# Output product of an FFN in two-row half-blocks: token combinations on another engine, plain rows in eight units, additions one unit later, rotary tables made in an earlier stage

## The chip, the cores and the metric

The kernel runs on one core of a Trainium2 chip. The metric is the time of one execution on the device in microseconds. A core has five engines that work side by side and wait for one another by semaphores: TensorE (PE, matrix products; PEld is its loading of weights), VectorE (DVE), ScalarE (ACT), GpSimd (POOL) and SyncE (SP, here used to issue transfers). Each runs its own instructions in order. Transfers between DRAM and the on-chip memory (SBUF) are issued by SP and, here, by POOL, and are carried out by DMA engines. Matrix products are summed up in PSUM, which is divided into banks; one bank holds a tile of 128 x 512 float32.

## What is computed

The reference is a trunk of two layers on x (512 tokens of 1024 float32 numbers). Layer 0 is a Conformer convolution module, layer 1 native sparse attention (queries, keys and values with a partial rotary embedding of the positions), and each is followed by a SwiGLU FFN of 2816 hidden numbers:

```python
x = x + conformer_conv_module(rmsnorm(x))
x = x + swiglu_ffn(rmsnorm(x))
x = x + nsa_attention(rmsnorm(x), positions)
x = x + swiglu_ffn(rmsnorm(x))

def swiglu_ffn(h, w_in, w_out):
    gate, up = jnp.split(h @ w_in, 2, axis=-1)
    return (jax.nn.silu(gate) * up) @ w_out
```

The rotary embedding takes the cosine and sine of `positions * inv_freq`, with `inv_freq = ROPE_THETA ** (-arange(8) / 8)`.

## The kernel before

Everything is kept transposed: x is eight tiles `x[m]` of 128 numbers by 512 tokens. A float32 product is made of three faster ones: each operand is split into a high part (rounded to the type fp32r) and the remainder, and high x high, high x low and low x high are summed in PSUM (`mm3`, lines 276 to 279). The weights are split on the chip: `next_w` (L229) asks for raw weights on SP's queue up to three units ahead (`w_dma`, L207; three buffers), ACT copies the high part (`w_hi`, L217), DVE subtracts it (`w_lo`, L226). High and low part have two buffers each, so a unit's split can be written only when the unit two before has been used.

The change is in the last stage of `ffn` (from L951), y times `w_out`. The 2816 rows of `w_out` are 22 blocks of 128. Eight of them, the plain rows (`EARLY` and `LATE`, four each), are multiplied as they stand. The other 14 are two halves of seven (`NO`), and with the two halves of the outputs and the two halves (256 tokens each) of the tokens they make a 2 x 2 block product, which the kernel forms with seven products in place of eight (Strassen's way). They come in the order `OUT_SEQ` = 1, 4, 2, 3, 5, 6, 7; each is 28 blocks of 128 x 128 weights, cut into four units u of 8, 8, 8 and 4 blocks, and a block is three matmuls of 256 columns. "(4,1)" below is unit 1 of product 4. Products 1, 4 and 7 use raw weights. The others use sums of two quarters of the weights, formed by DMA: `s_base` (L1029, SP's queue) loads one, `s_more` (L1033, POOL's queue) accumulates another upon it, and ACT and DVE split the sum (`soh` L1040, `sol` L1041).

The token operands are split too: `direct` (L992 to L996) for a quarter of y, `summed` (L1001, L1002) for a combination of quarters, which is formed by `z_1`, `z_4` (both through `z_new`, L1007) and `z_on` (L1020, in place), on POOL. `divide` (L757 to L761) splits the plain rows of y.

The results lie in PSUM. `bank()` hands out the six banks of the pool `fpm`; another pool, `fpa`, has two. For each of the four row blocks j of a product, `AD[j]` is a bank held from product 1 to product 7, `B[j]` one held during product 4. `out_add` (L1069 to L1076) adds a finished result to its half of x on DVE. When a tile of x is final, `finish_x` (L323) prepares the next layer: high part on ACT (L311), low part on DVE (L312), square on ACT, sum of the squares on POOL (the last on DVE).

The order is written out by hand. Plain rows come first: four units P0 to P3, each two tiles m by the four `EARLY` rows (`plain`, added to x by `keep_plain`, L962). The `LATE` rows are eight pieces of four blocks ("Q" slots), put between the units of the seven products by `LATE_AT` (L100) and made by `late` (L1118 to L1125) in a bank of `fpa`. `slots` lists the units, and the loop of L1142 does for each: ask for and split the weights of the next one, issue this unit's matmuls, do what `todo` lists for it (operands, transfers), then the additions that it has completed, and `finish_x`. Each engine keeps this order. The generator `rope_tables` (L1178) hands fourteen pieces of work on the rotary tables to the first FFN's `todo`: the load of the positions, DVE operations on 128 x 512 tiles and three ACT operations.

The convolution module ends with its own output product, for m = 0 to 7: addition to x (L719) and `finish_x`. The attention (`nsa`) takes the tables as arguments.

Of the kernel before, what the change touches and what calls it, by code (L numbers as in the profile page):

```python
# [19 lines left out]
P = 128  # L20
T = 512
# [78 lines left out]
LATE_AT = {(1, 1): (0,), (4, 0): (1,), (4, 2): (4,), (2, 0): (2,), (2, 2): (5,), (3, 0): (3,), (3, 2): (6,),  # L100
           (5, 1): (7,)}
# [16 lines left out]
def trunk(ctx: ExitStack, tc: tile.TileContext, A, out):  # L118
# [32 lines left out]
    def add_ffn(l):  # L151
# [5 lines left out]
        for i in range(4):  # L157
            add("fw_p", l * 4 + i, 1024)
        for z in OUT_SEQ:
            for u in range(QU):  # L160
                if z in OUT_RAW:
                    units.append(quarter(l, OUT_RAW[z], u))
                for m in LATE_AT.get((z, u), ()):
                    add("fw_r", l * NK + m, LATE * P)
# [221 lines left out]
    def proj_tile(pool, tag, xh=None, xl=None, mid=None, fixed=False):  # L386
# [16 lines left out]
        return ps  # L403


    def conv_module():
        acc = new_acc()
        with ExitStack() as cx:
# [307 lines left out]
            acc = new_acc()  # L716
            for m in range(NK):
                ps = pss[m] if m < 4 else proj_tile(po, "po", ah, al)
                nc.vector.tensor_tensor(x[m], x[m], ps, ALU.add)  # L719
                finish_x(m, V_NF0, acc, fin(m))  # L720
        return acc


    def ffn(acc, gnext, layer, between=None):
# [9 lines left out]
        with ExitStack() as cx:  # L734
# [219 lines left out]
            def plain(m):  # L954
                wh, wl = w
                pss[m] = bank()
                for f in range(EARLY):
                    c = slice(m % 2 * EARLY * P + f * P, m % 2 * EARLY * P + (f + 1) * P)
                    mm3(pss[m], wh[:, c], wl[:, c], ah[f], al[f], f == 0, f == EARLY - 1)
# [8 lines left out]
            plain(0)  # L968
# [35 lines left out]
            def z_new(name, g, a, b):  # L1004
                z = zs[name, g] = fo.tile([P, len(PAIRS[g]) * H], F32, tag=f"{name}{g}", name=nm("z"))
                for k, i in enumerate(PAIRS[g]):
                    pe(nc.gpsimd.tensor_tensor(z[:, k * H:(k + 1) * H], half(*a(i)), half(*b(i)), ALU.subtract))  # L1007
# [7 lines left out]
            def z_on(g, t, op):  # L1015
                z = zs["zz", g]
                for k, i in enumerate(PAIRS[g]):
                    c = slice(k * H, (k + 1) * H)
                    ab = (z[:, c], half(1, i, t)) if op == ALU.add else (half(1, i, t), z[:, c])
                    pe(nc.gpsimd.tensor_tensor(z[:, c], *ab, op))  # L1020
# [64 lines left out]
            tables = list(between(fo)) if between else []  # L1085
# [9 lines left out]
            for g in range(NG):  # L1095
                at(("P", (0, 1, 1, 2, 2)[g]), L(direct, 1, g, "oA", 0, 0, -1.0))
                at(("P", (1, 1, 1, 2, 2)[g]), L(z_1, g))
                at((1, (0, 0, 1, 1, 2)[g]), L(z_4, g))
# [19 lines left out]
            def late(m, w):  # L1118
                wh, wl = w
                ps = pa.tile([P, T], F32, tag="pa", name=nm("late"))  # L1120
                for k in range(LATE):
                    f = EARLY + k
                    c = slice(k * P, (k + 1) * P)
                    mm3(ps, wh[:, c], wl[:, c], ah[f], al[f], k == 0, k == LATE - 1)
                pe(nc.vector.tensor_tensor(x[m], x[m], ps, ALU.add))  # L1125

            slots = [("P", n) for n in range(1, 4)]
# [8 lines left out]
            plain(1)  # L1136
            keep_plain(0)
            for f in todo.pop(("P", 0)):
                f()
            keep_plain(1)  # L1140
            ready = None
            for n, (p, u) in enumerate(slots):  # L1142
# [877 lines left out]
```

## Time and profile before

| | |
|---|---|
| device time, three runs | 1276.36, 1276.45 and 1273.76 us, median 1276.36 |
| the profiled execution, its own time | 1270.59 us |
| its span, from the first to the last instruction | 1268.7 us |
| PE busy | 1211.6 us, 95% of the span |
| DVE busy | 916.5 us, 72% |
| ACT busy | 603.0 us, 48% |
| POOL busy | 413.9 us, 33% |
| output stage of the first FFN (417.70 to 552.40 us) | 134.70 us, PE busy 120.62, DVE 100.49, POOL 46.40 |
| output stage of the second FFN (1136.00 to 1265.40 us) | 129.40 us, PE busy 118.99, DVE 88.56, POOL 33.40 |

The profile belongs to one execution, which was faster than the three timed ones; its rows add up to its own time. An engine's busy time doesn't count instructions that only issue a transfer. "idle before <- X" in a row is the time that an engine stood before an instruction, with the instruction whose end released it. Numbers after an x are counts; "128x1024 fp32r<-128x1024 f32" is a tile written and a tile read, partitions by elements. L1063 is the matmul of `products`, `st` and `late` are PSUM tiles, `wl` and `wh` the low and high part of raw weights, `sol` and `soh` those of summed weights, `oz` a split token operand, `z` a combination of tokens, `al` and `ah` the parts of plain rows of y.

### The profile page before, as it was taken

What the parts mean: (1) busy time and instruction counts of PE and PEld (TensorE: products, weight loads), DVE (VectorE), ACT (ScalarE), POOL (GpSimd) and SP (SyncE); (2) the same over time, 40 slices, a digit from 0 to 9 for tenths busy, and PEclk for the clock granted to TensorE, in tenths of its full rate; (3) what the DMA queues carried; (4) which work ended last, traced back from release to release, by engine and by line L of the source; (5) the groups of instructions that cost most, each with busy time, mean ns of one, the idle gap of its engine ahead of it and who ended that gap; (6) DMA issues with size and microseconds to landing.
All of it is one profiled execution on the core that took longest, in us unless ns stands there. A gap on an engine that the chain in (4) does not pass through costs nothing.

```text
span 1268.7 us, 22185 instructions
## 1 busy us (share of the span) xinstructions
PE 1211.6 (95%) x8519; PEld 1047.5 (83%) x8519; DVE 916.5 (72%) x1604; ACT 603.0 (48%) x1124; POOL 413.9 (33%) x482
## 2 busy tenths in 40 slices
PE   9999999999999989889998999999999999998988
PEld 6787788899999888777777766668879999997878
DVE  6995678787666686755687887654597877767665
ACT  5221454455555344533443777753354544543433
POOL 2010030144443332332332566542212444442320
PEclk9999999999999999999999999999999999999999
DMA  8747635367774679154266011002534666638852
GB/s 312 259 147 257 174 111 160 112 170 211 186 181 127 182 200 182 26 171 114 58 143 167 18 34 26 3 15 68 184 105 142 175 175 174 175 104 224 197 124 84
DMA packets 89530, 180.06 MB, mean 142 GB/s; under 512 B 36880, under 2 KB 38544, under 8 KB 87888
## 3 DMA queue, kind: packets, MB, share of 16 engines
q1 hardware_dynamic: 68688, 112.48, 28.1%
q0 software_dynamic: 20736, 66.17, 23.2%
q8 instruction: 67, 1.10, 0.4%
q14 instruction: 39, 0.32, 0.1%
HBM read 165.08 MB, written 5.28 MB: 134 GB/s over the span
## 4 chain that ended last, share of the span: by engine, by line
PE 63%; DVE 12%; issue 10%; POOL 6%; ACT 4%; DMA 2%; SPq 2%; POOLq 0%; DVEq 0%; ACTq 0%
PE st L859 15%; PE st L1063 8%; PE pp L279 6%; PE pp L277 6%; PE pp L278 6%; PE O L1759 3%; PE cpe L515 2%; DVE wl L226 2%; POOL S L834 2%; PE pv L1594 2%; POOL S L833 2%; PE T L1733 1%; DVE sol L1041 1%; POOL S L826 1%; PE S L1702 1%
## 5 line engine op out<-in xcount | busy, mean ns | idle before, releaser
L217 ACT ACTIVATE wh<-wr 128x1024 fp32r<-128x1024 f32 (+3 forms) x158 | 154.2, 976 | 223.4 <-PE pp L278 60.8
L226 DVE TENSOR_TENSOR wl<-wr,wh 128x1024 fp32r<-128x1024 f32 (+3 forms) x158 | 186.6, 1181 | 32.0 <-ACT wh L217 31.4
L859 PE MATMUL st<-bh,sh 128*128 128x256 f32 x680 | 194.1, 285 | 3.5 <-DVE t L884 3.5
L859 PE MATMUL st<-bh,sl 128*128 128x256 f32 x680 | 192.5, 283 | 1.1 <-DVE sl L843 1.1
L859 PE MATMUL st<-bl,sh 128*128 128x256 f32 x680 | 192.0, 282 | 0.0
L277 PE MATMUL pp<-hh,wh 128*128 128x512 f32 x400 | 158.9, 400 | 3.7 <-ACT wh L217 3.6
L279 PE MATMUL pp<-hh,wl 128*128 128x512 f32 x400 | 157.6, 397 | 4.4 <-DVE wl L226 4.4
L278 PE MATMUL pp<-hl,wh 128*128 128x512 f32 x400 | 158.0, 396 | 0.0
L843 DVE TENSOR_TENSOR sl<-S,sh 128x512 fp32r<-128x512 f32 x136 | 111.8, 859 | 55.2 <-ACT sh L842 54.2
L859 PEld LDWEIGHTS st<-bh,sh 128*128 128x128 f32 x680 | 129.8, 191 | 5.8 <-DVE t L884 4.1
L859 PEld LDWEIGHTS st<-bh,sl 128*128 128x128 f32 x680 | 130.1, 191 | 1.5 <-DVE sl L843 1.5
L859 PEld LDWEIGHTS st<-bl,sh 128*128 128x128 f32 x680 | 130.5, 192 | 0.1
L1720 POOL TENSOR_SCALAR Pm<-Pm,sm,gates 128x512 f32<-128x512 f32 (+3 forms) x128 | 80.8, 643 | 59.9 <-DVE sm L1716 47.2
L833 POOL TENSOR_TENSOR S<-S,wr 128x512 f32<-128x512 f32 x34 | 53.9, 1586 | 134.1 <-DMA wr<-fw_in 71.6
L277 PEld LDWEIGHTS pp<-hh,wh 128*128 128x128 f32 x400 | 75.2, 188 | 24.6 <-ACT wh L217 6.0
L279 PEld LDWEIGHTS pp<-hh,wl 128*128 128x128 f32 x400 | 75.2, 188 | 24.0 <-DVE wl L226 6.9
L278 PEld LDWEIGHTS pp<-hl,wh 128*128 128x128 f32 x400 | 75.3, 188 | 18.0 <-issue 1.1
L842 ACT ACTIVATE sh<-S 128x512 fp32r<-128x512 f32 x136 | 79.2, 620 | 21.6 <-POOL S L833 21.5
L826 POOL DMA_DIRECT2D S<-fw_x x34 | 40.3, 1186 | 145.0 <-DMA S<-fw_x 143.9
L1706 ACT ACTIVATE Pm<-Pm,mx 128x512 f32<-128x512 f32 (+3 forms) x128 | 71.1, 557 | 34.1 <-DVE mx L1705 31.2
L1063 PE MATMUL st<-oz,soh 128*128 128x256 f32 x448 | 81.8, 284 | 0.5 <-ACT soh L1040 0.5
L1705 DVE CUSTOM_DVE_ANT_0 Pm<-S,mask 128x512 f32<-128x512 f32 (+3 forms) x128 | 59.2, 484 | 28.2 <-PE S L1703 27.6
(318 smaller groups left out, 3023.7 us busy)
## 6 DMA issues: line engine op xcount, KB each, us to landing
S<-fw_x POOLq DMA_DIRECT2D x68, 512.0 KB, 6.0
wr<-fw_in SPq DMA_DIRECT2D x46, 512.0 KB
bd<-bands POOLq DMA_DIRECT2D x12, 1280.0 KB, 12.8
So<-fw_q POOLq DMA_DIRECT2D x24, 512.0 KB, 5.9
wr<-fw_q SPq DMA_DIRECT2D x18, 512.0 KB
r<-fw_x SPq DMA_DIRECT2D x34, 256.0 KB
wr<-cw_in SPq DMA_DIRECT2D x14, 512.0 KB
So<-fw_q SPq DMA_DIRECT2D x12, 512.0 KB
```

Source lines behind the costliest of these rows:

```text
L217: parted(after(nc.scalar.activation(hi[:, :cols], raws[i][:, :cols], AF.Copy), pin.get(AF)))
L226: parted(after(nc.vector.tensor_tensor(lo[:, :cols], raws[i][:, :cols], hi[:, :cols], ALU.subtract), pin.get(ALU)))
L277: held(nc.tensor.matmul(ps, wh, xh, start=first, stop=False))
L278: held(nc.tensor.matmul(ps, wh, xl, start=False, stop=False))
L279: held(nc.tensor.matmul(ps, wl, xh, start=False, stop=last))
L833: pe(nc.gpsimd.tensor_tensor(t[:, :T], S[n][:, :T], w[:, :T], ALU.add))
L842: pe(nc.scalar.activation(h_[:, c], z, AF.Copy))
L843: pe(nc.vector.tensor_tensor(l_[:, c], z, h_[:, c], ALU.subtract))
L859: pe(nc.tensor.matmul(ps[:, :H], p_[:, k], m_[c][:, t], start=first and c == 0 and q == 0, stop=last and c == 3 and q == 2, skip_group_che ...
L1063: pe(nc.tensor.matmul(ps, a[:, c], b[:, t], start=p in (1, 4) and i == 0 and r == 0, stop=i == NO - 1 and r == 2, skip_group_check=True))
L1706: at_[AF] = nc.scalar.activation(Pt, Pt, AF.Exp, bias=mx, scale=-1.0, accum_out=sm)
L1720: nc.gpsimd.tensor_scalar(Pt, Pt, sm[:, k:k + 1], gates[:, t + k, br * 16 + h:br * 16 + h + 1], ALU.mult, ALU.mult)
```

## The change

1. `z_new` and `z_on` run on DVE: 28 operations of 128 x 256 per FFN.
2. The `late` pieces are gone. The plain rows are eight units of eight blocks (24 matmuls of 512): P0 has tiles 0 and 1 with rows 0 to 3, P1 tile 2 with rows 0 to 3 and tile 0 with rows 4 to 7, P2 tiles 1 and 2 with rows 4 to 7; then one unit for each tile 3 to 7 with all eight rows, placed by `PLAIN_AT` behind (4,1), (2,2), (3,0), (5,0) and (5,2). Each tile is added to x once, not twice: eight additions fewer per FFN. The weights are packed on the host to match. `divide` of rows 4 to 7 moves from P3 to P0.
3. Additions (`out_add`, `keep_plain`) are put into `behind` and issued one slot later, after the next unit's matmuls and `todo`; the last slot issues its own as well. `finish_x` follows them, and its sum of squares is on DVE.
4. `z_1` moves to P2, (1,0), (1,1), (1,2), `z_4` from product 1 to product 3, `direct` for product 1 to P1 and P2, half of the first `s_more` to (1,0).
5. The rotary tables are made in the output stage of the convolution module, three pieces after each of the tiles m = 3 to 7, in buffers of that stage (`uf`); the two results are written to DRAM (`angles`) and loaded again at the start of the attention. The positions and the two writes go by POOL's queue, the loads by SP's.

The PSUM pools and `bank()` are as before.

```diff
-LATE_AT = {(1, 1): (0,), (4, 0): (1,), (4, 2): (4,), (2, 0): (2,), (2, 2): (5,), (3, 0): (3,), (3, 2): (6,),
-           (5, 1): (7,)}
+PLAIN = [[(m, f) for m in range(a, b) for f in range(c, d)] for a, b, c, d in (
+    (0, 2, 0, 4), (2, 3, 0, 4), (0, 1, 4, 8), (1, 3, 4, 8), *((m, m + 1, 0, 8) for m in range(3, NK)))]
+PLAIN[1:3] = [PLAIN[1] + PLAIN[2]]
+PLAIN_AT = {(4, 1): 3, (2, 2): 4, (3, 0): 5, (5, 0): 6, (5, 2): 7}
...
+    angles = [tc.dram_tile([P, T], F32, name=nm("angle")) for _ in range(2)]
+
+    def rope_tables(new, follow):
+        pos = new(I32)
+        pf, n, sinT, cosT = (new(F32) for _ in range(4))
+        big = 1.5 * 2.0 ** 23
+        lim = 3.1415925
+
+        def g(name, *a):
+            return lambda: follow(getattr(nc.vector, name)(*a))
+
+        yield lambda: nc.gpsimd.dma_start(pos, A["positions"].partition_broadcast(P))
+        yield g("tensor_copy", pf, pos)
+        yield g("tensor_scalar", pf, pf, v(V_INVF), None, ALU.mult)
+        yield g("tensor_scalar", n, pf, 1.0 / (2.0 * math.pi), big, ALU.mult, ALU.add)
+        yield g("tensor_scalar", n, n, -big, None, ALU.add)
+        for c in _two_pi_pieces():
+            yield g("scalar_tensor_tensor", pf, n, -c, pf, ALU.mult, ALU.add)
+        yield g("tensor_scalar", pf, pf, lim, -lim, ALU.min, ALU.max)
+        yield lambda: (follow(nc.scalar.activation(sinT, pf, AF.Sin)), follow(nc.scalar.activation(n, pf, AF.Abs)),
+                       follow(nc.scalar.activation(cosT, n, AF.Sin, bias=halfpi, scale=-1.0)))
+        yield g("tensor_scalar", sinT, sinT, v(V_SGN), None, ALU.mult)
+        yield g("tensor_scalar", cosT, cosT, v(V_ISR), v(V_NISR), ALU.mult, ALU.add)
+        yield lambda: (nc.gpsimd.dma_start(angles[0], cosT), nc.gpsimd.dma_start(angles[1], sinT))
...
+            follow = dict(chain)
+
+            def table(dt):
+                return cp.tile([P, 8, 68], dt, tag="uf", bufs=len(PE_CONV), name=nm("tab")).rearrange(
+                    "p a b -> p (a b)")[:, :T]
+
+            tables = list(rope_tables(table, lambda z: after(z, follow[z.ins.engine])))
             for m in range(NK):
                 ps = pss[m] if m < 4 else proj_tile(po, "po", ah, al)
                 nc.vector.tensor_tensor(x[m], x[m], ps, ALU.add)
                 finish_x(m, V_NF0, acc, fin(m))
+                for _ in range(3 if m > 2 else 0):
+                    if tables:
+                        tables.pop(0)()
+            assert not tables
...
-            def plain(m):
+            def plain(w, blocks, k0=0):
                 wh, wl = w
-                pss[m] = bank()
-                for f in range(EARLY):
-                    c = slice(m % 2 * EARLY * P + f * P, m % 2 * EARLY * P + (f + 1) * P)
-                    mm3(pss[m], wh[:, c], wl[:, c], ah[f], al[f], f == 0, f == EARLY - 1)
+                for k, (m, f) in enumerate(blocks, k0):
+                    if m not in pss:
+                        pss[m] = bank()
+                    c = slice(k * P, (k + 1) * P)
+                    mm3(pss[m], wh[:, c], wl[:, c], ah[f], al[f], f == 0, f == EARLY + LATE - 1)
...
-                    pe(nc.gpsimd.tensor_tensor(z[:, k * H:(k + 1) * H], half(*a(i)), half(*b(i)), ALU.subtract))
+                    pe(nc.vector.tensor_tensor(z[:, k * H:(k + 1) * H], half(*a(i)), half(*b(i)), ALU.subtract))
...
-                    pe(nc.gpsimd.tensor_tensor(z[:, c], *ab, op))
+                    pe(nc.vector.tensor_tensor(z[:, c], *ab, op))
...
-                at(("P", (0, 1, 1, 2, 2)[g]), L(direct, 1, g, "oA", 0, 0, -1.0))
-                at(("P", (1, 1, 1, 2, 2)[g]), L(z_1, g))
-                at((1, (0, 0, 1, 1, 2)[g]), L(z_4, g))
+                at(("P", (1, 1, 2, 2)[g]), L(direct, 1, g, "oA", 0, 0, -1.0))
+                at((("P", 2), (1, 0), (1, 1), (1, 2))[g], L(z_1, g))
+                at((3, g), L(z_4, g))
...
-                at(("P", 3), L(divide, f, fo))
+                at(("P", 0), L(divide, f, fo))
...
-                at(("P", 2 + u // 2), L(s_more, 0, u))
+                at(("P", 2) if u < 2 else (1, 0), L(s_more, 0, u))
...
+            behind = []
+            slots = [("P", n) for n in range(1, 3)]
             for p in OUT_SEQ:
                 for u in range(QU):
                     slots.append((p, u))
-                    slots.extend(("Q", m) for m in LATE_AT.get((p, u), ()))
-            for n, f in enumerate(tables):
-                at(slots[1 + n], f)
+                    if (p, u) in PLAIN_AT:
+                        slots.append(("P", PLAIN_AT[p, u]))
...
-                if p == "Q":
-                    late(u, w)
-                    for f in todo.pop((p, u), ()):
-                        f()
-                    continue
+                sums_ = behind[:]
+                behind.clear()
                 if p == "P":
-                    plain(2 * u)
-                    plain(2 * u + 1)
-                    done = []
+                    plain(w, PLAIN[u])
+                    behind.extend(lambda m=m: keep_plain(m) for m, f in PLAIN[u] if f == EARLY + LATE - 1)
                 else:
-                    done = products(p, u, w)
+                    for j in products(p, u, w):
+                        behind.append(lambda p=p, j=j: out_add(p, j))
                 for f in todo.pop((p, u), ()):
                     f()
-                if p == "P":
-                    keep_plain(2 * u)
-                    keep_plain(2 * u + 1)
-                for j in done:
-                    out_add(p, j)
+                if n + 1 == len(slots):
+                    sums_ += behind
+                for f in sums_:
+                    f()
                 while finals:
                     m = finals.pop(0)
-                    finish_x(m, gnext, acc, fin(m))
+                    finish_x(m, gnext, acc, nc.vector)
...
+        tabs = []
+        for i in range(2):
+            t = rp.tile([P, T], F32, name=f"tab{i}")
+            nc.sync.dma_start(t, angles[i])
+            tabs.append(t)
+        cosT, sinT = tabs
...
-        fp.append(w[:EARLY].reshape(EARLY, P, 4, 2, P).transpose(2, 1, 3, 0, 4).reshape(4, P, 1024))
-        fr.append(w[EARLY:EARLY + LATE].transpose(2, 1, 0, 3).reshape(NK, P, LATE * P))
+        fp.extend(np.concatenate([w[f, :, m] for m, f in z], 1)[None] for z in PLAIN)
```

More of the change, by code (lines that the diff above doesn't have):

```diff
@@ L156, in add_ffn @@
             add("fw_in", l * n + i, 1024)
-        for i in range(4):
-            add("fw_p", l * 4 + i, 1024)
+        for i in range(3):
+            add("fw_p", l * NK + i, 1024)
         for z in OUT_SEQ:
@@ L162, in add_ffn @@
                     units.append(quarter(l, OUT_RAW[z], u))
-                for m in LATE_AT.get((z, u), ()):
-                    add("fw_r", l * NK + m, LATE * P)
+                if (z, u) in PLAIN_AT:
+                    add("fw_p", l * NK + PLAIN_AT[z, u], 1024)
     add_ffn(0)
@@ L720, in conv_module, with ffn @@
                 finish_x(m, V_NF0, acc, fin(m))
+                for _ in range(3 if m > 2 else 0):
+                    if tables:
+                        tables.pop(0)()
+            assert not tables
         return acc
-    def ffn(acc, gnext, layer, between=None):
+    def ffn(acc, gnext, layer):
         gcol = (V_NF0, V_NF1)[layer]
@@ L966, in split_next @@
                 w_lo()
-            plain(0)
+            plain(w, PLAIN[0][:4])
             split_next()
@@ L1083, in out_add @@
                     finals.append(m)
-            tables = list(between(fo)) if between else []
             NG = len(PAIRS)
@@ L1116, in ffn @@
                 at((4, u), L(s_more, 3, u))
[L1118 to L1127, printed above, removed]
+            behind = []
+            slots = [("P", n) for n in range(1, 3)]
             for p in OUT_SEQ:
@@ L1130, in ffn @@
                     slots.append((p, u))
-                    slots.extend(("Q", m) for m in LATE_AT.get((p, u), ()))
-            for n, f in enumerate(tables):
-                at(slots[1 + n], f)
+                    if (p, u) in PLAIN_AT:
+                        slots.append(("P", PLAIN_AT[p, u]))
             acc = new_acc() if gnext is not None else None
-            plain(1)
-            keep_plain(0)
+            plain(w, PLAIN[0][4:], 4)
             for f in todo.pop(("P", 0)):
                 f()
-            keep_plain(1)
             ready = None
@@ L1175, in ffn, with nsa @@
         return acc
-    rope = []
-    def rope_tables(fo):
+    def nsa(acc, gnext):
+        cx = ExitStack()
         rp = hx[0].enter_context(tc.tile_pool(name="rp", bufs=1))
-        cosT = rp.tile([P, T], F32, name="cosT")
-        sinT = rp.tile([P, T], F32, name="sinT")
-        rope.extend((cosT, sinT))
-        pf, n = (fo.tile([P, T], F32, name=z) for z in ("posf", "ropen"))
-        pos = fo.tile([P, T], I32, name="pos")
-        g = nc.vector
-        big = 1.5 * 2.0 ** 23
-        lim = 3.1415925
-        yield lambda: held(nc.sync.dma_start(pos, A["positions"].partition_broadcast(P)))
-        yield lambda: held(g.tensor_copy(pf, pos))
-        yield lambda: held(g.tensor_scalar(pf, pf, v(V_INVF), None, ALU.mult))
-        yield lambda: held(g.tensor_scalar(n, pf, 1.0 / (2.0 * math.pi), big, ALU.mult, ALU.add))
-        yield lambda: held(g.tensor_scalar(n, n, -big, None, ALU.add))
-        for c in _two_pi_pieces():
-            yield lambda c=c: held(g.scalar_tensor_tensor(pf, n, -c, pf, ALU.mult, ALU.add))
-        yield lambda: held(g.tensor_scalar(pf, pf, lim, -lim, ALU.min, ALU.max))
-        yield lambda: (held(nc.scalar.activation(sinT, pf, AF.Sin)), held(nc.scalar.activation(n, pf, AF.Abs)),
-                       held(nc.scalar.activation(cosT, n, AF.Sin, bias=halfpi, scale=-1.0)))
-        yield lambda: held(g.tensor_scalar(sinT, sinT, v(V_SGN), None, ALU.mult))
-        yield lambda: held(g.tensor_scalar(cosT, cosT, v(V_ISR), v(V_NISR), ALU.mult, ALU.add))
-    def nsa(acc, cosT, sinT, gnext):
-        cx = ExitStack()
+        tabs = []
[4 more added lines that the diff above has]
+        cosT, sinT = tabs
         def pool(cxx, name, bufs, **kw):
@@ L1856, in trunk @@
     cx0.close()
-    acc = ffn(acc, V_NM1, 0, rope_tables)
-    cosT, sinT = rope
-    acc = nsa(acc, cosT, sinT, V_NF1)
+    acc = ffn(acc, V_NM1, 0)
+    acc = nsa(acc, V_NF1)
     ffn(acc, None, 1)
@@ L1965, in _layout @@
     o["cw_os"], o["cw_o"] = start_units(co[:, :T]), tiles(co[:, T:])
-    fs, fi, fx, fp, fq, fr = [], [], [], [], [], []
+    fs, fi, fx, fp, fq = [], [], [], [], []
     for l in range(2):
@@ L1982, in _layout @@
     o["fw_s"], o["fw_in"], o["fw_x"] = np.concatenate(fs), np.concatenate(fi), np.concatenate(fx)
-    o["fw_p"], o["fw_q"], o["fw_r"] = np.concatenate(fp), np.concatenate(fq), np.concatenate(fr)
+    o["fw_p"], o["fw_q"] = np.concatenate(fp), np.concatenate(fq)
     w = f["nsa_w_in"][0]
```

## The prediction

> **What bounds the kernel now.** The execution whose page I read took 1270.59 us around this span:
> ```profile
> span 1268.7 us, 22185 instructions
> ```
> TensorE (PE) is nearly always busy, so a change pays only where PE waits. The change touches the output product of both FFNs (417–552 and 1136–1265 us) and the rotary tables. There I asked first for PE's waits by releaser (columns: total, count, longest), in the first FFN from 441 to 517, then from 517 to 556, then in the second FFN from 1160 to 1266:
> ```profile
> PE st L1063 <- DVE wl L226: 4.2, 2, 3.6
> PE st L1063 <- DVE sol L1041: 3.0, 3, 1.9
> ```
> ```profile
> PE st L1063 <- DVE sol L1041: 3.2, 3, 1.1
> PE st L1063 <- DVE wl L226: 2.0, 3, 0.9
> PE pp L279 <- DVE wl L226: 1.3, 1, 1.3
> PE pp L277 <- ACT wh L217: 1.1, 1, 1.1
> PE st L1063 <- ACT soh L1040: 0.5, 2, 0.3
> ```
> ```profile
> PE st L1063 <- DVE sol L1041: 5.7, 4, 4.0
> PE st L1063 <- DVE wl L226: 4.7, 3, 3.4
> ```
> All name the low half of a split weight, made on VectorE (DVE). Next the timeline at the longest waits (start, length, instruction, idle before). First FFN, start of product 1: PE, GpSimd (POOL), DVE:
> ```profile
> 448.29 0.58 PE L1063 MATMUL st<-oz,wl 128*128 128x256 f32 x1 [3.57 <-DVE wl L226]
> ```
> ```profile
> 439.21 5.20 POOL L1007 TENSOR_TENSOR z<-y,y 128x256 f32<-128x256 f32 x7
> ```
> ```profile
> 438.08 7.49 DVE L761 TENSOR_TENSOR al<-y,ah 128x512 fp32r<-128x512 f32 x4
> ```
> Second FFN, start of product 6:
> ```profile
> 1229.55 0.58 PE L1063 MATMUL st<-oz,sol 128*128 128x256 f32 x1 [3.99 <-DVE sol L1041]
> ```
> ```profile
> 1223.25 5.15 POOL L1020 TENSOR_TENSOR z<-y,z 128x256 f32<-128x256 f32 x7
> ```
> ```profile
> 1224.81 4.68 DVE L1041 TENSOR_TENSOR sol<-So,soh 128x1024 fp32r<-128x1024 f32 x1 [0.17 <-ACT soh L1040]
> ```
> Each time POOL combines operands while a DVE subtraction is stretched. What DVE operations take otherwise, from the groups of the first FFN's stage (last columns: busy, mean ns, idle before):
> ```profile
> L1041 DVE TENSOR_TENSOR sol<-So,soh 128x1024 fp32r<-128x1024 f32 x12 | 17.1, 1423 | 4.4 <-ACT soh L1040 4.4
> L226 DVE TENSOR_TENSOR wl<-wr,wh 128x1024 fp32r<-128x1024 f32 x12 | 15.3, 1274 | 5.0 <-ACT wh L217 5.0
> L1076 DVE TENSOR_TENSOR x<-x,st 128x256 f32<-128x256 f32 x27 | 11.1, 413 | 2.0 <-PE st L1063 2.0
> L226 DVE TENSOR_TENSOR wl<-wr,wh 128x512 fp32r<-128x512 f32 x11 | 9.1, 827 | 1.2 <-ACT wh L217 1.2
> L1002 DVE TENSOR_TENSOR oz<-z,oz 128x512 fp32r<-128x512 f32 x12 | 7.9, 681 | 0.0
> L761 DVE TENSOR_TENSOR al<-y,ah 128x512 fp32r<-128x512 f32 x4 | 7.5, 1932 | 0.0
> L1125 DVE TENSOR_TENSOR x<-x,late 128x512 f32<-128x512 f32 x8 | 5.5, 684 | 5.9 <-PE late L279 5.9
> ```
> `al` takes 1.93 us where a subtraction of that size takes 0.68, and one `sol` took 4.68 where the mean is 1.42. POOL needs 5.20/7 = 0.74 us per combination. The Trainium skill, "SBUF — State Buffer", section "SBUF: two separate sides", says that VectorE operations with two SBUF inputs and GpSimd operations that read SBUF exclude one another for a whole instruction, the loser blocking fully; the trace agrees in direction (1.93 against 0.68).
>
> The waits also cost clock. Windows of 15 us behind the waits of 3.4, 3.57 and 3.99 us (granted clock in the third column from the end, then DMA share):
> ```profile
> 1160.00:1175.00 15.00, 11.59 (x87) 10.84 (x86) 12.88 (x21) 5.45 (x12) 2.50 (x4) 1.00 0.84 256
> 448.00:463.00 15.00, 14.05 (x94) 13.30 (x95) 12.24 (x26) 4.74 (x7) 0.43 (x1) 0.89 0.88 255
> 1229.00:1244.00 15.00, 14.45 (x96) 13.73 (x96) 9.17 (x15) 4.50 (x7) 0.00 (x0) 0.89 0.25 87
> ```
> The chain of waits shows like units behind a slow and a normal start:
> ```profile
> 448.29 4.19 PE st L1063 x22
> ...
> 460.40 2.88 PE st L1063 x22
> ```
> So a slow clock costs 4.19 − 2.88 = 1.3 us, after 3.57 and 3.99, not after 3.4.
>
> **The change, part by part: what goes.** (1) The 28 combinations of an FFN move from POOL to DVE. PE's waits beside POOL fall: 3.57 and, at product 5 (longest of the `sol` waits, 1.9), down to the 0.5 that its two neighbours have ((3.0 − 1.9)/2): 1.4. Second FFN: 3.4, and 4.0 down to 0.5: 3.5. Together 11.9. (2) The two slow starts: 2.6. (3) The end of the first FFN: five wait groups of 8.1 us, in which the split of the new x (`finish_x`) stands ahead of weight splits. With additions and `finish_x` one unit later, the last unit's 0.9 and the next layer's 1.3 and 1.1 stay, others go but for about nothing: 8.1 − 3.3 = 4.8. In the last slot two tiles' `finish_x` fall together; I count 0 for that, at most the 0.8 of a subtraction. What goes: 19.3. (4) The matmuls stay, only cut into other units. Eight additions of 0.68 per FFN go, off PE's path, and make room for (1): a combination on DVE is 0.37 us by this row of the same shape:
> ```profile
> 208.16 0.75 DVE L796 TENSOR_TENSOR z<-z,z 128x256 f32<-128x256 f32 x2
> ```
> 28 × 0.37 = 10.5 against 8 × 0.68 = 5.5 and what the stretching cost: DVE's load stays about the same, and what matters is where it piles up. The sums of squares of `finish_x`, seven of 0.68 in the first FFN, come to DVE as well, behind the additions of products 5 and 7, where only splits a unit ahead follow; nothing, and 0.7 at the last tile if that cover is gone. The `divide` of four tiles goes from the fourth plain unit to the first: 4 × 0.68 = 2.7 us of DVE beside a unit of 24 matmuls of 512, 24 × 0.23 = 5.6 by the matmul row below; nothing, and 2.7 at most if the operands come late. The matmul row, from the chain of waits:
> ```profile
> 1169.27 0.23 PE late L277
> ```
>
> **What comes.** ACT's copy of a weight unit:
> ```profile
> L217 ACT ACTIVATE wh<-wr 128x1024 fp32r<-128x1024 f32 x13 | 13.7, 1057 | 29.8 <-PE st L278 15.1 <-PE st L1063 13.1 <-PE late L278 1.6
> ```
> (5) PSUM banks. `bank()` has six. In product 4 four hold AD, so two are left, and `late` no longer uses the other pool. An addition that frees a bank now runs behind the next unit's matmuls in the program, thus on DVE behind the split of the unit after it and that slot's operand work. Three places per FFN, counted from the end of the unit named:
> - B[2] begins 18 matmuls into (4,1): 18/24 of 2.88 = 2.2 us. It needs `out_add(4,0)`, behind ACT's copy for P3 (1.06), its `lo` (1.27), four combinations (1.5), one `summed` (0.68), and itself 0.41: 4.9. Stall 2.7.
> - P3 needs the bank of `out_add(4,1)`: 1.06 + 1.27 + 0.41. Stall 2.7.
> - B[3] begins 15 matmuls into (4,2), 1.8 us. It needs `keep_plain(3)`: short copy about 0.6 (half of 1.06, rounded up), `lo` 0.83, two combinations 0.75, half a `summed` 0.4, itself 0.68: 3.3. Stall 1.4 (1.5, less overlap).
> Sum 6.8, both FFNs 13.6. Bounds: 0 if the banks come free in time, 13.6 if the order holds as written. I take 13.6, because the order on DVE follows the program. What queues behind these additions is DVE's next split, which PE then doesn't wait for longer, since PE stands too.
>
> (6) Slot (1,0) gathers two combinations (0.75), four halves of `direct` (4 × 0.41, as the row of that size) and two plain additions (1.36): 3.8 us, and the split of (1,2) stands behind. A full unit runs 2.88; copy and `lo` take 2.3 of it. Beyond the slack of one unit I get 0.4 (start-to-start overlap of DVE's short operations) to 1.4; I take 0.9, both FFNs 1.8.
>
> (7) Transfers. The accumulates (`s_more`) are as many as before; but the POOL queue held them behind combinations that waited:
> ```profile
> POOL z L1020 <- DVE oz L1002: 16.5, 2, 14.9
> ```
> and an accumulate takes, from issue to landing,
> ```profile
> So<-fw_q POOLq DMA_DIRECT2D x24, 512.0 KB, 5.9
> ```
> Without that wait they go out as soon as their base has landed, up to 15 us earlier, into the stretch where DMA is already 0.88 busy (448–463). Raw weights are issued three units ahead; those of (4,1):
> ```profile
> 456.98 0.33 SPq L207 DMA_DIRECT2D wr<-fw_q  x1
> ```
> are needed at 460.40 + 2.88 = 463.3, 6.3 us later, hardly more than an accumulate's 5.9. The P phase is one unit shorter too (one of four full units moves behind). Bounds: 0, and 1.9 per FFN if the raw load for P3 becomes like an accumulate and its neighbour together; I take 1.0, the middle, since neither end has a nearer row: 2.0.
>
> (8) The rotary tables: 12 DVE operations move from the FFN into the convolution module's output stage, five of them at most of
> ```profile
> L1196 DVE SCALAR_TENSOR_TENSOR posf<-ropen,posf 128x512 f32<-128x512 f32 x5 | 4.3, 858 | 0.0
> ```
> so below 12 × 0.86 = 10.3 us, beside three copies on ACT, three per tile for m = 3..7. DVE stands idle there before its additions:
> ```profile
> 184.33 0.69 DVE L719 TENSOR_TENSOR x<-x,pp 128x512 f32<-128x512 f32 x1 [1.42 <-PE pp L279]
> ```
> ```profile
> 189.82 0.69 DVE L719 TENSOR_TENSOR x<-x,pp 128x512 f32<-128x512 f32 x1 [2.69 <-PE pp L279]
> ```
> and a tile takes 5.5 us, so three operations of 0.4–0.9 mostly fit (the rows start 5.5 us apart). Cover gone, the split of x for the next product is late: bounds 0 to 3 us, taken 0.5. The load of the positions and the two 256 KB writes go on the POOL queue, with only sums of squares behind them; the two reloads on SP's queue at the start of attention pass in front of weights already asked for, and are read only after the projections: nothing, and one transfer's 5.9 if that cover were gone.
>
> **Sum**: −19.3 + 13.6 + 1.8 + 2.0 + 0.5 = −1.4 us: 1269.2 against 1270.59. The median of the runs shown is 1276.36, 5.8 above the profiled one; so 1276.4 − 1.4 = 1275.0.
>
> **Rivals.**
> R1, *the banks don't bite*: additions are early enough, or a bank is free. For: all additions are short (0.41 to 0.68). Against: six banks, four held. −19.3 + 4.3 = −15.0: 1261.4.
> R2, *slower: the weights for P3 come late and the clock drops*. If they are over 0.8 us late, the 2.7 stall in (4,1) passes the 3.5 that lies between the waits without (3.4) and with (3.57) a slow start. Price: 1.9 in place of 1.0 per FFN (+1.8), and 1.3 per slow start, one or two per FFN (2.6 to 5.2): −1.4 + 4.4 = +3.0 to +5.6: 1279.4 to 1282. For: 6.3 us lead at a DMA share of 0.88. Against: PE's stall delays the need as well. The Trainium skill, "TensorE: Matmul & The Clock Gate", section "Part 1: The HAM clock gate (the "warmup" mystery)", lets the clock halve after a whole idle window of about 3.4 us that runs freely, by which a wait of 3.5 would seldom be enough and R2 would stay near +1; the trace, with 3.57 and 3.99 both slowed, leans the other way.
> R3, *the change doesn't do what it says*: `al` and `sol` are stretched by something other than POOL. Then 11.9 + 2.6 don't go: −1.4 + 14.5 = +13: 1289. Against: long only beside POOL.
>
> **How the numbers follow.** About 0.2%, 2.5 us, is what a measurement can tell. Forecast 0.50, own range −6 (smaller stalls in (5), a third of them gone) to +3 (the upper bounds of (6) and (8), and the 0.8 of (3)): 1270 to 1279. R1 0.21, R2 0.23, R3 0.06. Of the forecast's 0.50, 0.16 lies below −2.5, 0.30 within, 0.04 above; R2 gives 0.03 to "same". Faster 0.16 + 0.21 = 0.37; same 0.33; slower 0.04 + 0.20 + 0.06 = 0.30. The range 1260 to 1282 leaves out R3, R1's better part and R2's worst.
>
> **What would show it.** (1) right: `al` near 0.7, `sol` and `wl` near 1.25, no wait above 1 us at products 1, 5, 6 outside (5). (5) right: PE waits of 2 to 3 us within (4,1) and at P3, released by DVE `x` additions (L1076's and L962's successors). R1: none there. R2: ACT's copy for P3 waits for a DMA, clock below 0.95 around it. (8) wrong: PE waits in 185–240 us grow. The forecast fails if the DVE order differs from the program's, or if a queue no row shows turns late.

## The result, and the profile after

The changed kernel took 1284.8 us (median of 7 runs, 1279.23 to 1290.36) beside 1275.61 us for the kernel before (7 runs, 1272.73 to 1280.92): a ratio of 1.0072, 95% interval 1.0043 to 1.0101. It is slower, by 0.7%. The forecast was 1275.0 with a range of 1260 to 1282.

The profiled execution of the changed kernel was the slowest of its seven (1290.36 us), that of the kernel before was faster than all of its seven (1270.59), so the two profiles lie 19.8 us apart where the medians lie 9.2 apart. The views are read for where the time sits, not for the total. The page's first lines:

```profile
span 1288.6 us, 22113 instructions
## 1 busy us (share of the span) xinstructions
PE 1225.6 (95%) x8519; PEld 1057.7 (82%) x8519; DVE 905.9 (70%) x1642; ACT 601.9 (47%) x1116; POOL 359.7 (28%) x423
```

PE executes as many matmuls (8519) as before, but is "busy" 14 us longer, a first sign of a slower clock. PE's waits by releaser in the first FFN's output stage (425 to 560 us) and in the second's (from 1140 us):

```profile
PE st L1103 <- DVE x L1116: 3.5, 1, 3.5
PE st L1103 <- ACT wh L219: 3.2, 1, 3.2
PE st L1103 <- DVE sol L1081: 3.1, 5, 0.8
PE st L279 <- DVE x L1116: 2.6, 1, 2.6
PE st L1103 <- DVE wl L228: 2.4, 4, 0.7
PE st L1103 <- DVE x L1002: 1.1, 1, 1.1
```
```profile
PE st L1103 <- DVE x L1116: 3.5, 1, 3.5
PE st L1103 <- DVE wl L228: 2.7, 4, 0.8
PE st L1103 <- ACT wh L219: 2.7, 2, 2.3
PE st L279 <- DVE x L1116: 2.6, 1, 2.6
PE st L1103 <- DVE sol L1081: 2.3, 4, 0.7
PE st L1103 <- DVE x L1002: 1.0, 1, 1.0
```

The long waits for `wl` and `sol` are gone: none is above 0.8 us, where 1.9 to 4.0 stood before. In their place stand three waits for additions to x (L1116 is the line of `out_add`, L1002 that of `keep_plain`), one in front of B[2] (3.5), one in front of P3 (2.6) and one in front of B[3] (1.1). These are the three waits for a PSUM bank that the prediction named. A further one is for `wh`, the high part of the weights of (4,1): 3.2 us in the first FFN and 2.3 in the second.

Why the weights were late is seen on three engines. SP's timeline has the transfer's issue, ACT's the copy that waited for it:

```profile
448.53 0.33 SPq L209 DMA_DIRECT2D wr<-fw_q  x1
```
```profile
458.68 1.06 ACT L219 ACTIVATE wh<-wr 128x1024 fp32r<-128x1024 f32 x1 [6.29 <-DMA wr<-fw_q]
```

From the issue to the copy 10.2 us passed. In the kernel before, the transfer for the same unit went out at 456.98 us, and 6.2 us later the copy waited for PE, not for the transfer:

```profile
463.19 1.06 ACT L217 ACTIVATE wh<-wr 128x1024 fp32r<-128x1024 f32 x1 [2.09 <-PE st L1063]
```

In the changed kernel the weights of P3 came late as well. The addition that frees B[2] stands on DVE behind their split, so the wait of 3.5 us has late weights in it too:

```profile
463.73 1.06 ACT L219 ACTIVATE wh<-wr 128x1024 fp32r<-128x1024 f32 x1 [2.96 <-DMA wr<-fw_p]
```

POOL's timeline shows what ran beside the weights of (4,1), two accumulates for product 6:

```profile
447.66 0.85 POOL L1073 DMA_DIRECT2D So<-fw_q  x1 [0.64 <-DMA So<-fw_q]
450.73 0.85 POOL L1073 DMA_DIRECT2D So<-fw_q  x1 [2.22 <-DMA So<-fw_q]
```

Before the change only the first of the four had gone out by then; POOL then waited 14.9 us in front of a combination. The same stretch of the changed kernel in windows (start and end, length, busy time of PE, PEld, DVE, ACT and POOL, then the granted clock, third from the end, and the DMA share):

```profile
448.00:456.00 8.00, 6.79 (x55) 6.59 (x56) 5.34 (x12) 1.65 (x3) 1.37 (x2) 1.00 0.99 224
456.00:460.00 4.00, 0.79 (x6) 0.59 (x6) 0.23 (x1) 1.32 (x2) 0.00 (x0) 0.99 1.06 275
460.00:464.00 4.00, 3.46 (x16) 3.17 (x16) 2.52 (x4) 1.04 (x3) 0.85 (x1) 0.50 1.02 351
464.00:472.00 8.00, 2.47 (x10) 1.89 (x9) 4.56 (x8) 2.37 (x3) 0.85 (x1) 0.50 0.83 218
472.00:477.00 5.00, 4.36 (x10) 3.47 (x11) 0.49 (x2) 0.00 (x0) 0.00 (x0) 0.50 0.35 108
```

The DMA engines are full from 448 to 464 us (shares of 0.99 to 1.06), PE is busy for 2.5 of the eight microseconds after 464, and from 460 to 477 us the clock is granted at half. In the kernel before, the clock of this stage fell once, to a mean of 0.89 over 448 to 463 us. DVE itself was relieved. Its groups in this stage:

```profile
L228 DVE TENSOR_TENSOR wl<-wr,wh 128x1024 fp32r<-128x1024 f32 x16 | 19.6, 1223 | 21.4 <-ACT wh L219 21.4
L1081 DVE TENSOR_TENSOR sol<-So,soh 128x1024 fp32r<-128x1024 f32 x12 | 14.7, 1224 | 15.4 <-ACT soh L1080 15.3
```
```profile
L800 DVE TENSOR_TENSOR al<-y,ah 128x512 fp32r<-128x512 f32 x4 | 2.5, 685 | 0.0
```

The mean of `al` fell from 1.93 to 0.69 us, that of `sol` from 1.42 to 1.22. In the kernel before, the mean of 1.93 was made of three subtractions of 0.68 us and one that lasted as long as POOL's seven combinations beside it (5.20 us from 439.21):

```profile
439.28 5.68 DVE L761 TENSOR_TENSOR al<-y,ah 128x512 fp32r<-128x512 f32 x1
```

So the mechanism that the change is built on works, and what it gained was lost elsewhere. One more place: the convolution module's output stage, where PE waits once for a split, and windows of 180 to 184 us before and after:

```profile
PE pp L281 <- DVE wl L228: 1.9, 1, 1.9
```
```profile
180.00:184.00 4.00, 4.00 (x19) 3.29 (x18) 2.91 (x2) 0.84 (x2) 1.49 (x2) 1.00 0.66 224
```
```profile
180.00:184.00 4.00, 2.12 (x9) 1.70 (x9) 4.00 (x5) 2.19 (x3) 2.07 (x1) 0.93 0.25 67
```

The table operations fill DVE (4.00 of 4.00 us against 2.91), and PE stands.

### The profile page after: what moved, and what is told of

Same layout as the page of the kernel before. It is cut to its first block, busy times and chain, and to the rows that moved or that the text cites. A ratio compares the mean times of both kernels' runs of the same rounds, so it can differ in the third digit from the quotient of the medians.

```text
span 1288.6 us, 22113 instructions
## 1 busy us (share of the span) xinstructions
PE 1225.6 (95%) x8519; PEld 1057.7 (82%) x8519; DVE 905.9 (70%) x1642; ACT 601.9 (47%) x1116; POOL 359.7 (28%) x423
## 5 line engine op out<-in xcount | busy, mean ns | idle before, releaser
L228 DVE TENSOR_TENSOR wl<-wr,wh 128x1024 fp32r<-128x1024 f32 (+3 forms) x150 | 183.9, 1226 | 73.4 <-ACT wh L219 73.2
L898 PEld LDWEIGHTS st<-bh,sh 128*128 128x128 f32 x680 | 129.9, 191 | 1.2 <-DVE t L923 0.5
L881 ACT ACTIVATE sh<-S 128x512 fp32r<-128x512 f32 x136 | 79.2, 620 | 14.9 <-POOL S L872 14.7
L1073 POOL DMA_DIRECT2D So<-fw_q x32 | 27.5, 868 | 187.7 <-DMA So<-fw_q 96.1
```

What stands on the lines that cost most here:

```text
L228: parted(after(nc.vector.tensor_tensor(lo[:, :cols], raws[i][:, :cols], hi[:, :cols], ALU.subtract), pin.get(ALU)))
L881: pe(nc.scalar.activation(h_[:, c], z, AF.Copy))
L898: pe(nc.tensor.matmul(ps[:, :H], p_[:, k], m_[c][:, t], start=first and c == 0 and q == 0, stop=last and c == 3 and q == 2, skip_group_che ...
```

## The experiments

To keep chance between launches out, each profile was also cut into stages (in us) by PE's timeline. "Conv" runs from the start of the convolution module's output product to the first half-block matmul of the first FFN's input product; "FFN 0" and "FFN 1" run from the first matmul of P0 to the last of product 7. Ratios are to the kernel before, run beside each on the same chip, with 95% intervals; these, and not the medians, compare kernels. A stage time belongs to one execution: kernels whose second FFN has the same program differ in it by up to 1.3 us, and since the changed kernel's profile was its slowest run, differences against its row come out larger than by the ratios.

| kernel | median us | ratio | conv | FFN 0 | FFN 1 |
|---|---|---|---|---|---|
| before | 1275.61 | 1 | 103.3 | 133.5 | 129.3 |
| changed | 1284.8 | 1.0072 [1.0043, 1.0101] | 107.2 | 139.8 | 138.7 |
| e_banks | 1267.52 | 0.9968 [0.9942, 0.9994] | 105.8 | 129.9 | 126.7 |
| e_late_sums | 1272.63 | 1.0021 [0.9997, 1.0046] | 105.8 | 133.1 | 132.2 |
| e_both | 1257.05 | 0.9895 [0.9854, 0.9936] | 107.3 | 124.2 | 122.0 |
| e_now | 1276.39 | 1.0035 [1.0007, 1.0063] | 107.3 | 136.7 | 133.4 |
| e_both_pool | 1269.36 | 0.9976 [0.9948, 1.0004] | 105.8 | 129.1 | 130.9 |
| e_both_now | 1257.0 | 0.9875 [0.9833, 0.9917] | 107.3 | 125.7 | 121.7 |
| e_acc_pool | 1261.95 | 0.9908 [0.9875, 0.9940] | 107.3 | 127.0 | 122.9 |
| e_z_alone | 1264.11 | 0.9935 [0.9908, 0.9962] | 103.3 | 133.1 | 125.9 |
| e_tab | 1281.23 | 1.0063 [1.0040, 1.0086] | 103.3 | 139.3 | 137.4 |
| e_both_tab | 1248.38 | 0.9800 [0.9743, 0.9857] | 103.2 | 123.7 | 122.3 |
| e_both_2 | 1253.59 | 0.9835 [0.9799, 0.9871] | 107.4 | 124.3 | 122.4 |
| e_best | 1254.73 | 0.9842 [0.9806, 0.9877] | 103.3 | 125.6 | 122.4 |

My theory after the result: the wait for banks and the late weights each cost, and together they bring the clock down. The first rival was that transfers alone decide and the bank waits only hide them.

**e_banks.** The two banks of the other pool, idle since the change, are used for B[0], B[1] and B[3]; B[2] keeps its own:

```diff
-                    B[j] = bank()
+                    B[j] = bank() if j == 2 else pa.tile([P, T], F32, tag="pa", name=nm("st"))
```

> The changed kernel, but B[0], B[1] and B[3] lie in the second PSUM pool, whose two banks the change left idle, so that no matmul of product 4 and no plain unit waits for an addition. Theory (late weights and the wait for banks each cost, and together they drop the clock): PE's waits for x additions (3.5, 2.6 and 1.1 us per FFN) go, the weights of (4,1) stay late by 2 to 4 us and those of the next plain unit become late by about 2; the time falls by 12 to 18 us against the changed kernel, to about 1270. Rival 1 (transfers alone decide, the bank waits only hide them): the waits move to the weights of P3 and (4,2), and the time falls by less than 5, to 1280 or more. Rival 2 (the slow clock comes from something else): the clock stays near 0.985.

Against the changed kernel the ratio falls by 0.0104, some 13 us, and the mean clock of the runs is 0.990 to 0.995 in place of 0.981 to 0.989, so rival 2 falls. PE waits no more for additions. The weights of (4,1) stay late, by 1.5 us in the second FFN and by 3.4 in the first, and the clock is still at half for 3.4 and 6.8 us there:

```profile
PE st L1103 <- ACT wh L219: 3.4, 1, 3.4
```

PE does not wait for the weights of P3, though the theory had expected it to.

**e_late_sums.** The sums that only product 6 needs are asked for later:

```diff
-                at((1, u), L(s_base, 3, u))
-                at((4, u), L(s_more, 3, u))
+                at((2, u), L(s_base, 3, u))
+                at((3, u), L(s_more, 3, u))
```

> The changed kernel, but the sums for product 6 (s_base and s_more of index 3: eight transfers, 3.5 MB per FFN) are asked for in products 2 and 3, not in products 1 and 4; nothing else. Theory: the weights of (4,1) come in time, the three bank waits stay at 3.5, 2.6 and 1.1 us, the clock drops less long; the time falls by 6 to 11 us against the changed kernel, to 1274 to 1279. Rival 1 (transfers alone decide): it falls by 15 or more, below 1270. Rival 3 (the weights are late because they are asked for late, the first plain units being shorter): the wait for the weights of (4,1) stays above 2 us and the time within 3 us of the changed kernel.

The ratio falls by 0.0051, some 6.5 us, at the theory's lower end. No wait for `wh` is left in the stage; raw weights are asked for at the same point of the program as in the changed kernel, so rival 3 falls: what made them late was what shared the DMA engines with them. The bank waits, freed from the rest, in the first FFN, and the clock there from 459 to 469 us:

```profile
PE st L279 <- DVE x L1116: 2.6, 1, 2.6
PE st L1103 <- DVE x L1116: 2.5, 1, 2.5
```
```profile
459.00:469.00 10.00, 7.38 (x21) 5.87 (x22) 1.56 (x2) 1.06 (x1) 0.00 (x0) 0.52 0.20 68
```

and in the second FFN:

```profile
PE st L1103 <- DVE x L1116: 2.8, 1, 2.8
PE st L279 <- DVE x L1116: 2.6, 1, 2.6
```

This is the reading that mattered most: no wait is longer than 2.8 us, and still the clock is at half for 10.2 us in each FFN.

**e_both.** Both edits.

> Both edits together. Theory: neither the bank waits nor the late weights remain, no half-speed clock in either FFN's output stage; the time falls by 24 to 30 us against the changed kernel, to 1255 to 1261, so the move of the combinations to VectorE and the later additions are worth about 15 us by themselves. Rival 4 (the move to VectorE itself costs, by piling up work on it): waits for wl or sol grow where the bank waits went, and the time stays at 1268 or more.

The ratio falls by 0.0177, some 22.6 us, a little under the 24 to 30 expected (30 in e_both_2, the same kernel once more), and the kernel is faster than the one before. The two FFN stages take 246.2 us together against 278.5 in the changed kernel and 262.8 before. All of PE's longer waits in the first FFN's stage are these; the clock there is full:

```profile
PE st L1103 <- DVE sol L1081: 3.1, 5, 0.8
PE st L1103 <- DVE wl L228: 2.6, 4, 0.8
```

The two edits alone bring 21.9 and 13.2 us in these stages, 35.1 by addition, together 32.3. So neither hides the other, and the first rival falls.

**e_now.** Additions in their own slot, nothing else: every slot runs `sums_ + behind`.

> The changed kernel, but additions are issued in their own slot, as before the change. Theory: no wait for a bank longer than about 1 us, but the weights of (4,1) stay late by 2 to 3 us, and the waits at the end of the first FFN come back (about 5 us); the time falls by 6 to 12 us against the changed kernel, to 1273 to 1279. Rival 1 (transfers alone): within 3 us of the changed kernel.

The ratio falls by 0.0037, some 5 us, a little less than the theory said, and not in its way. P3 waits even longer for an addition, and of the waits at the end of the first FFN only 1.6 us came back (5.1 against 3.5 in the last 36 us of the stage and the 6 us behind it). PE, then ACT:

```profile
467.75 0.76 PE L279 MATMUL st<-ah,wh 128*128 128x512 f32 x1 [5.33 <-DVE x L1116]
```
```profile
463.01 1.06 ACT L219 ACTIVATE wh<-wr 128x1024 fp32r<-128x1024 f32 x1 [5.26 <-DMA wr<-fw_p]
```

The addition that frees the bank stands on DVE behind the split of P3's own weights, and the copy could take these only at 463. A releaser named "addition" was a late transfer, two steps further back. Such a wait is to be followed to the head of the queue of the engine named.

**e_both_pool.** e_both with the combinations back on GpSimd.

> The kernel with both edits (banks and later sums), but the token combinations back on GpSimd. Theory (GpSimd's combinations stretch VectorE's subtractions, which is what the change removes): al is made before GpSimd combines, so the first place is spared, but sol or wl beside z is stretched again to 2 to 4.7 us somewhere in products 4 and 5, with PE waits of 2 to 4 us; the time is 5 to 14 us above the kernel with both edits. Rival 4 (the move to VectorE only shifts load and isn't worth anything): within 3 us.

The ratio is 0.0081 above that of e_both, some 10 us (0.0141 above that of e_both_2); the FFN stages take 260.0 us against 246.2. POOL and DVE in the first FFN, and the wait of PE that follows:

```profile
499.42 7.50 POOL L1060 TENSOR_TENSOR z<-y,z 128x256 f32<-128x256 f32 x7
```
```profile
499.57 5.12 DVE L1081 TENSOR_TENSOR sol<-So,soh 128x1024 fp32r<-128x1024 f32 x1 [0.51 <-ACT soh L1080]
```
```profile
PE st L1103 <- DVE sol L1081: 7.0, 5, 4.5
```

So the stretch is caused by POOL's combinations: moved back, they bring it back. The Trainium skill, "SBUF — State Buffer", section "SBUF: two separate sides", states an exclusive lock held for a whole instruction; the trace agrees that DVE stands while POOL works, but a DVE subtraction of 1.22 us beside seven short POOL operations takes 5.12, and one of 0.68 in the kernel before took 5.68, so here it lost its turn to several of them.

**e_both_now, e_acc_pool.** e_both with additions in their own slot; then also with the sums of squares on GpSimd (`fin(m)` in place of `nc.vector`).

> The kernel with both edits, but additions in their own slot. As the prediction had it, the later additions are worth about 5 us at the end of the first FFN: then the time is 4 to 6 us above the kernel with both edits. Rival 5 (what shortened the end of the first FFN was the work taken from GpSimd, not the later additions): PE's waits there stay below 6 us and the time is within 3 us.

> Both edits and additions in their own slot, but the sums of squares on GpSimd as before. Rival 5 (what shortened the end of the first FFN is the work taken from GpSimd): splits beside GpSimd's sums become longer (1.5 us in place of 1.23), PE's waits between 510 and 560 us grow by 1 to 3 us against the same kernel with the sums on VectorE, the time by as much. Otherwise (the longer plain units give the slack): no change within 1 us of wait.

The ratios can't tell these three kernels apart: 0.9895, 0.9875 and 0.9908, with intervals that overlap. The end of the first FFN does. In the last 36 us of its stage and the 6 us behind it PE's waits are 3.3 us in e_both and 3.5 in e_both_2, 5.2 with additions in their own slot (5.6 in e_best, further down), and 7.3 with the sums of squares on GpSimd as well; 8.2 stood before the change. The first FFN's stage takes 124.2 and 124.3 us, then 125.7 (125.6 in e_best), then 127.0. So each of the two steps is worth 1.3 to 1.5 us of stage, near the edge of what one execution can tell. The 1.2 us by which e_acc_pool is also longer in the second FFN are chance, since no layer follows there and no sum of squares is made. DVE and POOL at one place of e_acc_pool:

```profile
529.98 1.52 DVE L1081 TENSOR_TENSOR sol<-So,soh 128x1024 fp32r<-128x1024 f32 x1 [0.72 <-ACT soh L1080]
```
```profile
529.08 1.33 POOL L323 TENSOR_TENSOR acc<-acc,sq 128x512 f32<-128x512 f32 x1 [5.64 <-ACT sq L321]
```

The two overlap from 529.98 to 530.41 us, and the split takes 1.52 us where it takes 1.22 alone. So rival 5 holds for about half of what the end of the first FFN gained, and the prediction's reason for a good third.

**e_z_alone.** The kernel before, with `nc.vector` in place of `nc.gpsimd` in `z_new` and `z_on`, nothing else.

> The kernel before, with the 28 combinations per FFN moved to VectorE and nothing else. Theory: the waits of 3.6, 3.4, 1.9 and 4.0 us shrink and the clock drops go, but the combinations z_1, still in the plain units, stand in front of al, and the accumulates for product 6 go out early into the busy stretch, so weights of product 4 may be late by 1 to 3 us: 4 to 10 us below the kernel before, 1264 to 1270. Rival 4: within 3 us of the kernel before, or above it.

The ratio is 0.9935, some 8 us faster than the kernel before, as the theory had it. In the profile the FFN stages are 3.8 us shorter, 3.4 of it in the second; the rest of the 7.4 us between the two profiles lies in stages that the edit does not touch. In the second FFN PE's waits are

```profile
PE st L1063 <- DVE wl L226: 2.3, 4, 0.8
PE st L1063 <- DVE sol L1041: 2.3, 4, 0.7
PE st L1063 <- ACT wh L217: 1.9, 1, 1.9
```

where 5.7 and 4.7 stood. The wait for late weights, 1.9 us, appears here too, with none of the change's other parts. The second accumulate for product 6 in this kernel (33.0 us after the first matmul of P0), then in the kernel before (47.0 us after it), and the copy for (4,1) in this one:

```profile
1164.98 0.86 POOL L1033 DMA_DIRECT2D So<-fw_q  x1 [1.07 <-DMA So<-fw_q]
```
```profile
1182.89 0.85 POOL L1033 DMA_DIRECT2D So<-fw_q  x1
```
```profile
1176.59 1.06 ACT L217 ACTIVATE wh<-wr 128x1024 fp32r<-128x1024 f32 x1 [4.68 <-DMA wr<-fw_q]
```

Taking the combinations from POOL's queue is thus enough to let the accumulates out early and to make weights late.

**e_tab, e_both_tab, e_both_2, e_best.** The tables go back into the first FFN's output stage, one piece per unit from (4,3) on, upon the changed kernel, upon e_both, and upon e_both_now; e_both once more beside the last.

> The changed kernel, but the rotary tables are made in the first FFN's output stage, one piece per unit from (4,3) on; banks and sums as in the change. Theory: the 1.9 us wait and the clock drop in the convolution module's output stage go, the rest stays: 3 to 5 us below the changed kernel. Rival 6 (the 9 us that the same edit brought upon the two others came mostly from chance differences between launches, or only where the banks are free): within 2 us of the changed kernel.

> The kernel with both edits, but the rotary tables are made in the first FFN's output stage again, one piece per unit from (4,3) on, where transfers are fewer than in product 1; no tables by way of DRAM. Theory: the wait of 1.9 us in the convolution module's output stage and the half-speed clock behind it go, and the pieces (0.4 to 0.9 us each) fit between VectorE's splits: 2 to 4 us below the kernel with both edits. Rival 6 (the tables cost as much there): within 1 us of it.

> The kernel with both edits once more, beside the next one on one chip, for the size of what the tables cost: 1255 to 1260, ratio to the kernel before 0.987 to 0.991.

> Both edits, tables in the first FFN as in the kernel with tables moved back, and additions in their own slot. Theory (the later additions are worth nothing once the banks are free; the tables cost 4 to 9 us in the convolution module): 4 to 9 us below the kernel with both edits, 1246 to 1253, ratio 0.978 to 0.984. If the later additions do matter beside the table operations: 1253 or more.

The conv stage shows it clearly: 103.2 to 103.3 us with the tables elsewhere, 105.8 to 107.4 with them in the convolution module; the 1.9 us wait, and in most launches one dip of the clock behind it. The totals do not settle what that is worth, and the theory's 4 to 9 us did not show: 0.9800 and 0.9842 without, 0.9895 and 0.9835 with, 1.0063 against 1.0072 upon the changed kernel. The intervals overlap, launches of one kernel differ by several microseconds in stages that no edit touched (the first FFN's input product took 169.6 us in most profiles and 173.2 in that of e_both), and the 8.7 us between the medians of e_both and e_both_tab, which ran on two chips, were not found again between e_both_2 and e_best on one (though e_best also has its additions in their own slot). What is shown is 2.5 to 4 us of stage. The fastest kernels, at 0.980 to 0.990 of the kernel before, faster than both, have the combinations on VectorE, B in both pools, and the sums for product 6 asked for late.

## Why the prediction was wrong, point by point

**Right: step (1) and (2).** 11.9 + 2.6 = 14.5 us were forecast for taking the combinations from GpSimd. e_both_pool against e_both gives 13.8 in the two stages, 9.1 of it waits and the rest clock. That the sums agree so well is partly luck: `z_1` and `z_4` had moved, so the places are others. The prediction also took 1.93 us for the time of one stretched `al`; it is the mean of one of 5.68 and three of 0.68. Two slips in its working carry nothing: 24 × 0.23 is 5.5, not 5.6, and not all waits listed name a low half (1.1 and 0.5 us name ACT's high half).

**Right: the waits of step (5).** Forecast 2.7, 2.7 and 1.4 per FFN; undisturbed (e_late_sums) they were 2.5, 2.6, 1.1 and 2.8, 2.6, 1.1. Reading the bank count and DVE's order from the program gave them to 0.3 us. R1, that the banks would not bite, is refuted for the changed kernel. Its figure, 15.0 us below the kernel before, is what the change is worth with the banks mended and the transfers nearly so: e_both and e_both_2 are 13 and 21 us below (ratios 0.9895 and 0.9835 of 1275.6).

**Wrong in size: the clock behind step (5).** The prediction let the clock drop only behind a single wait above 3.5 us. With waits of 2.5 and 2.6 us, 4 us apart, it was at half for ten, where each of the single waits of 3.57 and 3.99 us in the kernel before had brought 3.4 us at half. The stages of e_late_sums are 265.3 us against 246.2 in e_both; 12.7 of these 19.1 are the waits themselves, about 6 the clock. The Trainium skill, "TensorE: Matmul & The Clock Gate", section "Part 1: The HAM clock gate (the "warmup" mystery)", asks for a whole idle window of about 3.4 us; the dips here come in steps of that length, 3.41 us, but no wait in e_late_sums was that long, so the measurement decides against taking that length as a safe limit.

**Wrong in size: step (7), the largest error.** 2.0 us were put down, the middle between 0 and 1.9 per FFN. e_late_sums against the changed kernel gives 13.2 us in the stages and 6.5 by the ratios, e_both against e_banks 10.4 and 9.3. The weights were not 1.0 us late but 3.2 and 2.3 (3.4 and 1.5 with the banks free), and it was (4,1), not P3, that was late first. The upper bound was the error. It counted one neighbour's transfer, and the 1.9 is worked out from no row; the DMA engines were full for at least 16 us, and a raw load took 10.2 us there. The lead before the change, 6.3 us, was read, and that a raw load could take 10 was not considered. With this term alone taken away, in e_late_sums, the ratio is 1.0021 and its interval holds 1, near the small change that had been forecast. It is not the only term that turns the sign: e_banks, with the weights still late, is at 0.9968.

**R2 is nearly what happened.** It had late weights, a longer stall and a dropping clock, at 1279.4 to 1282. Its signs were there: ACT's copy for P3 waited 2.96 us for its transfer, and the clock around it was at half. But the unit ahead of P3, (4,1), was late first, and the price was too small, because it took the clock's loss as 1.3 us per start where the profile has 17 us at half in the first FFN and, in the second, a mean of 0.67 from 1180 to 1200 us. It had a chance of 0.23; its row of the DMA share, 0.88, spoke for it more than I let it.

**Right in size, half wrong in cause: step (3).** 4.8 us were forecast from later additions and `finish_x`. The waits at the end of the first FFN fell by 4.7, from 8.2 to 3.5. Of these about 1.7 came from the later additions, about 2.1 from the sums of squares taken from GpSimd, which the prediction had put at nothing, and 0.9 from the rest. That the sum agrees is luck.

**Right: step (6).** Forecast 0.9 per FFN; the waits at the starts of (1,2) were 0.59 in both FFNs, a little less. **Too small: step (8).** 0.5 was forecast, with bounds of 0 and 3; the stage took 2.5 us more, and with the dip of the clock 4. The two reloads of the tables were not issued at the start of the attention but at 429 us, in the first FFN's output stage. They did not make the weights late: in e_tab, without them, PE waits 2.2 us for those of (4,1).

**Sum.** In the FFN stages the forecast was −19.3 + 13.6 + 1.8 + 2.0 = −1.9 us; the profiles show 278.5 − 262.8 = +15.7. The difference of 17.6 is the transfers (13.2 in place of 2.0) and the clock behind the bank waits (about 6). The medians missed the forecast by less, +9.2 us in place of −1.4: the profile of the changed kernel was its slowest run and that of the kernel before a fast one, so the sizes here are upper ones, and the ratios give the lower ones (6.5 to 9.3 us for the transfers).

## What to carry to other kernels

When work leaves an engine whose queue also issues transfers, its waits were a throttle. Count which transfers will now start earlier, and whether the stretch that they move into is already full. When an addition that frees a PSUM bank is put off, count live banks at each allocation; here the wait could be read from the program to 0.3 us, and an idle bank in another pool may cure it. Two middling waits close together can cost more in clock than one long one, so price stalls in a stretch, not one by one.

## What was not expected of the hardware

The clock fell to half without any wait of 3.4 us: behind one wait of 1.9 us (convolution module, in the profiles of the changed kernel, e_both, e_both_now and others, though not in e_banks, e_late_sums and e_both_pool, which have the same wait), and behind 2.5 + 2.6 us. In the changed kernel it stayed there for 17 us, with the bank waits of 3.5 and 2.6 us inside. What decides between a dip and none for one and the same wait was not tried. Nor was it tried which of the eight transfers moved in e_late_sums, the loads or the accumulates, did the harm.
